# Groups of seven products: the seventh product's weight split issued behind the third product's

## The chip, the cores and the metric

The kernel runs on one core of one Trainium2 chip. The metric is device time in microseconds (us) of one execution; lower is better. A profiled execution of the kernel before is shown below, and times are compared as medians.

## The reference

One layer of a hybrid encoder, 256 rows by 2048 columns, all float32: a half-weight SwiGLU block, a mixing block (a diagonal state-space head group and a stick-breaking attention head group side by side), a second half-weight SwiGLU block, and a gated per-layer embedding.

```python
x = x + 0.5 * swiglu(rms_norm(x, ffn1_norm), w_gate, w_up, w_down)      # d_ff = 5632
h = rms_norm(x, mix_norm);  u, q, k, v = split(h @ w_in)
x = x + concat(rms_norm(s5(u)), rms_norm(attention(q, k, v))) @ w_out
x = x + 0.5 * swiglu(rms_norm(x, ffn2_norm), ...)
x = x + rms_norm((p @ w_ple_proj) * sigmoid(rms_norm(x, ple_norm) @ w_ple_gate))

def swiglu(h, w_gate, w_up, w_down):
    return (silu(h @ w_gate) * (h @ w_up)) @ w_down
```

The change touches only the two SwiGLU blocks.

## The kernel before

**Matrix products in two halves.** Each float32 weight tile is split into a high part (a cast on ScalarE, line 181) and a low part (source minus high part, on VectorE, line 184). A product is then three runs of matmuls on TensorE: high activations with high weights, low with high (lines 494 and 495 for a product of a group), and high with low (line 497). Each weight tile of a split is 128 partitions by 1024 elements and serves six matmuls of 128x512 in a group's product: four that need the high part, then two that need the low part. In the ordinary blocks (`gemm_half`, lines 322, 323 and 327) one split serves twelve.

**Groups of seven products.** For most of the two SwiGLU blocks, `Seven.chunk` computes a 2 by 2 block product (two halves of the contraction by two column blocks) with seven products instead of eight. It loads two raw weight tiles, `raw` (line 511), whose halves are b11, b21 (first tile) and b12, b22 (second tile). VectorE forms three sums (line 501): t1 = b11 + b12, t2 = t1 + b22, t4 = t2 + b21. A transfer issued by GpSimd (line 525) adds b22 onto b12 in place, in on-chip memory; it may start only after t1 has read b12. The products are then traced in this order: 1 (weights b11), 5 (t1), 6 (t2), 4 (t4), 2 (b21), 3 (b22), 7 (b12 after the transfer). So the seventh product's split waits for the transfer, and the fourth product's split waits for the last sum. The kernel has 40 such groups; the text numbers them 1 to 40 by the transfers of line 525 in order of time. "P4" is the product numbered 4 of a group, and so on.

**What sets the order.** The code traces instructions; a scheduler then puts each engine's instructions into one fixed order, and each engine works that list strictly in order, waiting at the head of it. Weight parts go through small rings of buffers: four pairs `whi`/`wlo`, and in these phases three pairs `shi`/`slo`, used in turn (`weight_pair`, line 284). Between groups, `column` computes ordinary quarter products (its matmuls are those of lines 322, 323 and 327), and `step()` lets side work go on (line 592: a copy from an accumulator; lines 593, 594, 598, 601, 627 and 629: the combination of the seven accumulators and the gate; line 216: a transposition).

## Time and profile before

| | before |
|---|---|
| median of 3 runs | 1828.03 us (1827.74 to 1829.2) |
| the profiled execution's own time | 1829.07 us |
| its span, first to last instruction | 1827.3 us |
| TensorE matmuls busy | 1817.7 us (99%) |
| VectorE busy | 1518.4 us (83%) |
| ScalarE busy | 1048.0 us (57%) |
| mean granted TensorE clock | 0.998 |

Busy time of matmuls includes overlap: one 128x512 matmul is shown as lasting 0.39 us, while the next one starts 0.23 us after it. A gap of TensorE is therefore read from the starts of its rows, not from its busy share. A row of the timeline gives the start, the duration, engine, line, operation, output <- input, shape and count, and in brackets the idle time before it and what ended that.

### The profile page before, as it was taken

How to read it: one execution, taken by the hardware profiler on the slowest of the kernel's cores; microseconds unless marked ns; L12 is line 12 of the kernel's file. 1: busy time of each engine (PE TensorE's matmuls, PEld its weight loads, DVE VectorE, ACT ScalarE, POOL GpSimd, SP SyncE). 2: the span in 40 equal slices, each digit the busy share in tenths (PEclk: the TensorE clock that was granted, in tenths of full speed). 3: DMA queues.
4: the chain of work that ended last, by engine and by line, in shares of the span. 5: the costliest groups of instructions: out<-in, count | busy, mean ns of one | idle time of the engine just before them, and what ended most of it. 6: DMA issues, size and time to landing. Idle time of an engine off the chain costs nothing.

```text
span 1827.3 us, 24177 instructions
## 1 busy us (share of the span) xinstructions
PE 1817.7 (99%) x8954; PEld 1504.9 (82%) x8954; DVE 1518.4 (83%) x1773; ACT 1048.0 (57%) x1220; POOL 101.0 (6%) x156
## 2 busy tenths in 40 slices
PE   9999999999999999999999999999999999999998
PEld 7888888888888888888898888888878888888887
DVE  8966759999898885697567899999989999888565
ACT  7444445655565665456695566555555556556554
POOL 0010000000000001010021000000000010000000
PEclk9999999999999999999999999999999999999999
DMA  9899877787777677674646788887777787667563
GB/s 328 282 286 281 247 226 231 235 246 220 254 246 238 189 250 229 186 252 156 220 149 213 241 280 234 265 258 222 241 220 236 237 274 241 226 202 250 172 217 127
DMA packets 234407, 425.27 MB, mean 233 GB/s; under 512 B 24272, under 2 KB 48240, under 8 KB 234128
## 3 DMA queue, kind: packets, MB, share of 16 engines
q1 hardware_dynamic: 223872, 390.06, 64.9%
q0 software_dynamic: 9696, 32.25, 8.1%
q8 instruction: 70, 1.15, 0.3%
q10 hardware_dynamic: 720, 1.41, 0.2%
q14 instruction: 49, 0.40, 0.1%
HBM read 372.41 MB, written 10.88 MB: 210 GB/s over the span
## 4 chain that ended last, share of the span: by engine, by line
PE 98%; DMA 1%; DVE 0%; ACT 0%; issue 0%; SPq 0%; ACTq 0%; DVEq 0%
PE acc L322 18%; PE acc L323 18%; PE acc L327 18%; PE aux L323 7%; PE aux L327 7%; PE aux L322 7%; PE acc L497 4%; PE acc L495 4%; PE acc L494 4%; PE aux L497 3%; PE aux L495 3%; PE aux L494 3%; DMA raw<-raw 1%; PE aux L1142 0%; PE acc L1398 0%; PE acc L1393 0%
## 5 line engine op out<-in xcount | busy, mean ns | idle before, releaser
L184 DVE TENSOR_TENSOR wlo<-raw,whi 128x1024 fp32r<-128x1024 f32 x486 | 589.0, 1224 | 179.3 <-ACT whi L181 177.9
L181 ACT CAST whi<-raw 128x1024 fp32r<-128x1024 f32 x486 | 505.3, 1050 | 352.5 <-PE acc L323 234.7
L322 PE MATMUL acc<-whi,nhi 128*128 128x512 f32 x1052 | 412.4, 392 | 0.9 <-ACT whi L181 0.4
L323 PE MATMUL acc<-whi,nlo 128*128 128x512 f32 x1052 | 409.6, 389 | 0.0
L327 PE MATMUL acc<-wlo,nhi 128*128 128x512 f32 x1052 | 288.8, 389 | 0.0
L184 DVE TENSOR_TENSOR slo<-raw,shi 128x1024 fp32r<-128x1024 f32 x180 | 219.2, 1218 | 32.7 <-ACT shi L181 31.3
L322 PEld LDWEIGHTS acc<-whi,nhi 128*128 128x128 f32 x1052 | 197.6, 188 | 43.9 <-ACT whi L273 1.4
L181 ACT CAST shi<-raw 128x1024 fp32r<-128x1024 f32 x180 | 188.7, 1050 | 76.1 <-DMA raw<-in_ffn_w_down 22.8
L327 PEld LDWEIGHTS acc<-wlo,nhi 128*128 128x128 f32 x1052 | 197.5, 188 | 41.1
L323 PEld LDWEIGHTS acc<-whi,nlo 128*128 128x128 f32 x1052 | 197.6, 188 | 40.1
L181 ACT CAST whi<-sum 128x1024 fp32r<-128x1024 f32 x68 | 71.6, 1053 | 136.5 <-DVE sum L501 129.9
L181 ACT CAST shi<-sum 128x1024 fp32r<-128x1024 f32 x52 | 54.8, 1053 | 85.4 <-DVE sum L501 83.0
L501 DVE TENSOR_TENSOR sum<-sum,raw 128x1024 f32<-128x1024 f32 x80 | 97.6, 1220 | 0.7
L525 POOL DMA_DIRECT2D raw<-raw x40 | 34.7, 868 | 955.3 <-DVE sum L501 657.6
L184 DVE TENSOR_TENSOR wlo<-sum,whi 128x1024 fp32r<-128x1024 f32 x68 | 83.1, 1221 | 2.4 <-ACT whi L181 1.6
L184 DVE TENSOR_TENSOR slo<-sum,shi 128x1024 fp32r<-128x1024 f32 x52 | 63.5, 1221 | 2.4 <-ACT shi L181 1.9
L322 PE MATMUL aux<-whi,hhi 128*128 128x512 f32 x168 | 65.4, 389 | 0.0
L323 PE MATMUL aux<-whi,hlo 128*128 128x512 f32 x168 | 65.4, 389 | 0.0
L323 PE MATMUL acc<-whi,hlo 128*128 128x512 f32 x160 | 62.3, 390 | 0.0
L322 PE MATMUL acc<-whi,hhi 128*128 128x512 f32 x160 | 62.2, 389 | 0.0
L322 PE MATMUL aux<-whi,nhi 128*128 128x512 f32 x156 | 60.7, 389 | 0.0
L323 PE MATMUL aux<-whi,nlo 128*128 128x512 f32 x156 | 60.7, 389 | 0.0
(375 smaller groups left out, 3200.2 us busy)
## 6 DMA issues: line engine op xcount, KB each, us to landing
raw<-in_ffn_w_up SPq DMA_DIRECT2D x88, 1024.0 KB, 6.1
raw<-in_ffn_w_down SPq DMA_DIRECT2D x88, 1024.0 KB, 5.3
raw<-in_ffn_w_gate SPq DMA_DIRECT2D x86, 1024.0 KB, 8.0
raw<-in_w_in SPq DMA_DIRECT2D x32, 1024.0 KB, 5.8
raw<-raw POOLq DMA_DIRECT2D x40, 512.0 KB, 5.9
raw<-in_w_out SPq DMA_DIRECT2D x16, 1024.0 KB, 5.2
raw<-in_w_ple_gate SPq DMA_DIRECT2D x16, 1024.0 KB, 5.3
hT<-mid SPq DMA_DIRECT2D x160, 64.0 KB, 4.3
```

Source lines behind the costliest of these rows:

```text
L181: copy = nc.scalar.copy(hi, src)
L184: nc.vector.tensor_tensor(out=lo, in0=src, in1=hi.bitcast(F32), op=ALU.subtract)
L322: nc.tensor.matmul(ps[t], lhsT=lh, rhs=hi[:, j, cols], start=start and j == 0, stop=False)
L323: nc.tensor.matmul(ps[t], lhsT=ll, rhs=hi[:, j, cols], start=False, stop=False)
L327: nc.tensor.matmul(ps[t], lhsT=lh, rhs=lo[:, j, cols], start=False, stop=stop and j == 1)
L494: nc.tensor.matmul(ps, lhsT=lh[j], rhs=hi[:, j], start=begin and j == 0, stop=False)
L495: nc.tensor.matmul(ps, lhsT=ll[j], rhs=hi[:, j], start=False, stop=False)
L497: nc.tensor.matmul(ps, lhsT=lh[j], rhs=lo[:, j], start=False, stop=z in final and j == 1)
L501: nc.vector.tensor_tensor(out=t, in0=x, in1=y, op=ALU.add)
L525: nc.gpsimd.dma_start(b12, b22, accum_op=ALU.add)
```

## The change

`split` now returns its two instructions, `product` keeps them, and `chunk` takes those of the third product and traces the seventh product inside two blocks that put the instructions of ScalarE behind the third product's cast and those of VectorE behind the third product's subtraction. Nothing is computed differently; the number of instructions on each engine is the same.

```diff
     def split(hi, lo, src, scale=None, pinned=False):
         if scale is None:
             copy = nc.scalar.copy(hi, src)
...
-            nc.vector.tensor_tensor(out=lo, in0=src, in1=hi.bitcast(F32), op=ALU.subtract)
+            rest = nc.vector.tensor_tensor(out=lo, in0=src, in1=hi.bitcast(F32), op=ALU.subtract)
+            return copy.ins, rest.ins
...
         def product(self, z, left, src, final):
             hi, lo = weight_pair()
-            split(hi, lo, src)
+            self.last = split(hi, lo, src)
...
             self.product(2, whole(1, 0), b21, final)
             self.product(3, summed(3), b22, final)
+            copied, rest = self.last
             step()
-            self.product(7, summed(2), b12, final)
+            with tc.issue_after(copied), tc.issue_after(rest):
+                self.product(7, summed(2), b12, final)
```

In 35 of the 40 groups ScalarE cast the seventh product's weights behind the third's already. The final order differs in few places: ScalarE's in groups 1, 15, 24, 28 and 29 and (one cast and one copy exchanged) behind group 31, VectorE's around groups 1, 24, 28 and 29, TensorE's in groups 24 and 28. GpSimd's and SyncE's orders are the same throughout.

Group 29, ScalarE, before. Here `raw_11502` in `shi_11571<-raw_11502` is b12 (P7), `sum_11539` is t4 (P4), and `whi_11561<-raw_11502` reads b22 (P3); `shi_11551` is P2 and `sum_11527` is t2 (P6).

```order
L181 CAST shi_11551<-raw_11500 128x1024
L181 CAST whi_11529<-sum_11527 128x1024
L181 CAST shi_11571<-raw_11502 128x1024
L181 CAST whi_11541<-sum_11539 128x1024
L181 CAST whi_11561<-raw_11502 128x1024
L181 CAST whi_11583<-raw_11581 128x1024
```

The same place now:

```order
L181 CAST shi_11551<-raw_11500 128x1024
L181 CAST whi_11529<-sum_11527 128x1024
L181 CAST whi_11541<-sum_11539 128x1024
L181 CAST whi_11561<-raw_11502 128x1024
L181 CAST shi_11571<-raw_11502 128x1024
L181 CAST whi_11583<-raw_11581 128x1024
```

P7's cast moved from ahead of P4's and P3's to behind both. VectorE's subtractions `slo_11572`, `wlo_11542` and `wlo_11562` moved in the same way.

Group 1, ScalarE, before: `whi_2687` is P2, `whi_2708` is P7, `whi_2720` belongs to the ordinary product that follows, `shi_2677` is P4 and `shi_2697` is P3.

```order
L181 CAST whi_2664<-sum_2662 128x1024
L181 CAST whi_2687<-raw_2633 128x1024
L181 CAST whi_2708<-raw_2635 128x1024
L181 CAST whi_2720<-raw_2718 128x1024
L181 CAST shi_2677<-sum_2675 128x1024
L181 CAST shi_2697<-raw_2635 128x1024
```

The same place now:

```order
L181 CAST whi_2664<-sum_2662 128x1024
L181 CAST whi_2687<-raw_2633 128x1024
L181 CAST shi_2677<-sum_2675 128x1024
L181 CAST shi_2697<-raw_2635 128x1024
L181 CAST whi_2708<-raw_2635 128x1024
L181 CAST whi_2720<-raw_2718 128x1024
```

P4's and P3's casts moved ahead of P7's and of the following product's. On VectorE, P7's subtraction moved behind those of P4 and P3.

Group 24, VectorE, before: `wlo_10742` is P2, `slo_10731` is P4, `slo_10753` is P3; the two rows of `h_10349` combine the column block before.

```order
L501 TENSOR_TENSOR sum_10728<-sum_10715,raw_10686 128x1024
L627 TENSOR_TENSOR h_10349<-aux_10420,h_10349 128x1024
L184 TENSOR_TENSOR wlo_10742<-raw_10686,whi_10741 128x1024
L629 SCALAR_TENSOR_TENSOR h_10349<-h_10349,sm_9066,sg_10348 128x512 x2
L184 TENSOR_TENSOR slo_10731<-sum_10728,shi_10730 128x1024
L184 TENSOR_TENSOR slo_10753<-raw_10688,shi_10752 128x1024
```

The same place now (three lines further on in the file after the edited ones):

```order
L502 TENSOR_TENSOR sum_10728<-sum_10715,raw_10686 128x1024
L630 TENSOR_TENSOR h_10349<-aux_10420,h_10349 128x1024
L184 TENSOR_TENSOR slo_10731<-sum_10728,shi_10730 128x1024
L632 SCALAR_TENSOR_TENSOR h_10349<-h_10349,sm_9066,sg_10348 128x512 x2
L184 TENSOR_TENSOR wlo_10742<-raw_10686,whi_10741 128x1024
L184 TENSOR_TENSOR slo_10753<-raw_10688,shi_10752 128x1024
```

P4's and P2's subtractions have changed places. Group 28 reads the same with other numbers, and in both groups TensorE's two matmuls on P4's low part, which stood behind the first matmul of P2, now stand ahead of it.

## The prediction

> **What bounds the kernel now.** I read the page first, parts 1 and 4.

> ```profile
> PE 1817.7 (99%) x8954; PEld 1504.9 (82%) x8954; DVE 1518.4 (83%) x1773; ACT 1048.0 (57%) x1220; POOL 101.0 (6%) x156
> ...
> PE 98%; DMA 1%; DVE 0%; ACT 0%; issue 0%; SPq 0%; ACTq 0%; DVEq 0%
> ```

> The chain that ended last is TensorE's own work for 98% of the span. No matmul is added or removed, so the change can give back only time in which TensorE stood still or ran slowly, and can cost only by making it stand still somewhere. Second view: who TensorE waited for.

> ```profile
> PE acc L494 <- ACT whi L181: 1.9, 1, 1.9
> ...
> PE aux L497 <- DVE wlo L184: 0.4, 1, 0.4
> ```

> The longest wait of the execution is a single one, 1.9 us for a cast on ScalarE. Third view: TensorE's timeline, searched for starts that lie further apart than usual. Around that wait (group 29) it reads:

> ```profile
> 1339.58 0.39 PE L494 MATMUL acc<-whi,hhi 128*128 128x512 f32 x1
> ...
> 1343.21 0.61 PE L497 MATMUL aux<-wlo,nhi 128*128 128x512 f32 x2
> 1345.70 0.50 PE L494 MATMUL acc<-whi,hhi 128*128 128x512 f32 x1 [1.87 <-ACT whi L181]
> ...
> 1347.14 1.22 PE L497 MATMUL acc<-wlo,hhi 128*128 128x512 f32 x2 [0.25 <-DVE wlo L184]
> ...
> 1350.65 0.39 PE L494 MATMUL aux<-whi,nhi 128*128 128x512 f32 x1
> ...
> 1353.40 0.39 PE L322 MATMUL aux<-whi,nhi 128*128 128x512 f32 x1
> ```

> From 1339.58 to 1343.21 sixteen matmuls start, so the undisturbed distance is 3.63/16 = 0.227 us. From 1343.21 to 1353.40 there are 26 starts (two of P6, six each of P4, P2, P3, P7), which should take 26 x 0.2267 = 5.89 us and took 10.19. Group 29 therefore loses **4.30 us**, far more than the 1.9 us in the table of waits: 2.57 us up to 1347.14 (3.93 us for six starts worth 1.36), and 1.73 us after it. The second piece is the clock. Busy time by stretch, with the granted clock in the column behind the count:

> ```profile
> 1343.40:1347.10 3.70, 1.63 (x6) 1.00 0.44 161
> 1347.10:1350.50 3.40, 3.35 (x8) 0.50 0.27 42
> ```

> Right behind the stall TensorE is granted half its clock for 3.4 us, and gets eight matmuls done where fifteen would fit.

> Why the cast was late is on ScalarE's and VectorE's timelines:

> ```profile
> 1335.62 1.06 ACT L181 CAST whi<-sum 128x1024 fp32r<-128x1024 f32 x1 [0.19 <-DVE sum L501]
> 1343.65 1.04 ACT L181 CAST shi<-raw 128x1024 fp32r<-128x1024 f32 x1 [6.97 <-DMA raw<-raw]
> 1344.60 1.04 ACT L181 CAST whi<-sum 128x1024 fp32r<-128x1024 f32 x1
> 1345.55 1.99 ACT L181 CAST whi<-raw 128x1024 fp32r<-128x1024 f32 x2
> ```

> ```profile
> 1338.92 1.22 DVE L501 TENSOR_TENSOR sum<-sum,raw 128x1024 f32<-128x1024 f32 x1
> 1344.73 1.23 DVE L184 TENSOR_TENSOR slo<-raw,shi 128x1024 fp32r<-128x1024 f32 x1 [4.59 <-ACT shi L181]
> 1345.87 1.22 DVE L184 TENSOR_TENSOR wlo<-sum,whi 128x1024 fp32r<-128x1024 f32 x1
> 1347.01 2.36 DVE L184 TENSOR_TENSOR wlo<-raw,whi 128x1024 fp32r<-128x1024 f32 x2
> ```

> ScalarE stood 6.97 us at the head of its list, before P7's cast, until the adding transfer had landed. P4's cast, the next in the list, had its source (t4) at 1338.92 + 1.22 = 1340.14, but ran at 1344.60. VectorE stood 4.59 us for the same reason.

> **Group 29, the first term.** ScalarE's list now has P4, P3, P7. P4's cast can start at about 1340.2 and end at 1341.2; TensorE wants it at 1343.21 + 2 x 0.2267 = 1343.66. VectorE's subtraction then ends at about 1342.5; its first matmul is due four starts later, at 1344.57. P3's cast ends at about 1342.2 and is due at 1346.38. So P4 has a cover of 2.4 and 2.1 us, and the 4.30 us go. What is late next is P7 itself: its cast still waits for the transfer until 1343.65 and ends at 1344.69, its subtraction ends at 1344.73 + 1.23 = 1345.96; due at 1347.74 and 1348.65, so 3.05 and 2.69 us are left. Behind the waiting cast stand the next ordinary product's casts. They used to start behind three casts from 1343.65, and now start behind one, 1.9 us earlier. If the transfer lands over 2.7 us later than here, TensorE waits for the excess.

> Is the landing an accident of this execution? Part 6 of the page, and the adding transfer of the stretch 1333 to 1345 alone:

> ```profile
> raw<-raw POOLq DMA_DIRECT2D x40, 512.0 KB, 5.9
> ```

> ```profile
> DMA to landing us min/median/max: 9.5/9.5/9.5
> ```

> 9.5 us against a median of 5.9: the transfer was slow here. Weight loads go out ahead of it from SyncE's fixed list, so I expect much the same in every execution. But a landing about 2 us earlier would leave little of the stall, and that is a rival below.

> [...]

> **Group 1, the second term.** The same fault, milder:

> ```profile
> 292.87 0.61 PE L497 MATMUL aux<-wlo,hhi 128*128 128x512 f32 x2
> 293.44 0.50 PE L494 MATMUL acc<-shi,nhi 128*128 128x512 f32 x1
> ...
> 294.71 0.74 PE L497 MATMUL acc<-slo,nhi 128*128 128x512 f32 x2
> ...
> 296.65 0.39 PE L494 MATMUL aux<-shi,hhi 128*128 128x512 f32 x1
> ```

> ```profile
> 290.44 2.00 ACT L181 CAST whi<-raw 128x1024 fp32r<-128x1024 f32 x2 [1.31 <-PE acc L495]
> 292.35 1.04 ACT L181 CAST shi<-sum 128x1024 fp32r<-128x1024 f32 x1
> ```

> ```profile
> 289.35 1.22 DVE L501 TENSOR_TENSOR sum<-sum,raw 128x1024 f32<-128x1024 f32 x1
> ```

> 292.87 to 296.65 is 3.78 us for 14 starts worth 3.17: **0.61 us** lost. P4's cast (292.35) ended at 293.39, just before its matmul. Two casts stood ahead of it that now stand behind; t4 is ready at 290.57, so the cast can end at about 291.65, the subtraction at 292.9, against dues of 293.33 and 294.23. Covers of 1.7 and 1.3 us: all 0.61 us go. P7's cast moves from 290.44 to about 292.6, and is used from about 297.4 on.

> **The other moved places, at nothing.** In group 15 P7's cast, which waited for a buffer, goes behind P4's and P3's; in group 31 one cast passes the copy of line 592.

> ```profile
> 1043.30 1.05 ACT L181 CAST whi<-raw 128x1024 fp32r<-128x1024 f32 x1 [1.49 <-PE aux L327]
> ```

> ```profile
> 1048.40 1.22 DVE L184 TENSOR_TENSOR wlo<-raw,whi 128x1024 fp32r<-128x1024 f32 x1
> ...
> 1394.40 0.69 DVE L593 TENSOR_TENSOR h<-aux,sg 128x512 f32<-128x512 f32 x1 [2.12 <-PE aux L497]
> ```

> P7's cast in group 15 can be later by two casts (1.9 us) and still end at about 1046.3, ahead of its subtraction at 1048.40. The copy's reader in group 31 (line 593) waits 2.12 us for TensorE anyway, which covers the one cast. Should either cover be gone, the lateness beyond it is TensorE's. Group 24 (28 is its twin) moves P2's subtraction back:

> ```profile
> 1240.02 1.41 DVE L629 SCALAR_TENSOR_TENSOR h<-h,sm,sg 128x512 f32<-128x512 f32 x2
> 1241.35 1.22 DVE L184 TENSOR_TENSOR slo<-sum,shi 128x1024 fp32r<-128x1024 f32 x1
> ```

> ```profile
> 1243.92 0.61 PE L497 MATMUL acc<-wlo,hhi 128*128 128x512 f32 x2
> ```

> P2's low part now takes the slot at 1241.35 and ends at 1242.57; its matmuls are at 1243.92. Cover 1.35 us; without it every late microsecond is one of TensorE's. P4's low part takes P2's earlier slot. Its cast no longer stands behind P7's, so nothing is lost there.

> **What is given back.** TensorE moves ahead by 4.30 us in group 29; VectorE doesn't. From 1345.96 on VectorE works without a break, and only the two subtractions now done ahead of P7's (2 x 1.14 = 2.27 us) are saved, and a short gap in group 30 (its P7 subtraction is the row at 1370.44, its first matmul the one at 1373.35):

> ```profile
> 1363.15 1.22 DVE L184 TENSOR_TENSOR slo<-raw,shi 128x1024 fp32r<-128x1024 f32 x1
> 1364.48 1.22 DVE L627 TENSOR_TENSOR h<-aux,h 128x1024 f32<-128x1024 f32 x1
> ...
> 1370.44 1.18 DVE L184 TENSOR_TENSOR wlo<-raw,whi 128x1024 fp32r<-128x1024 f32 x1
> ```

> ```profile
> 1373.35 0.62 PE L497 MATMUL aux<-wlo,nhi 128*128 128x512 f32 x2
> ```

> Line 627 starts 1.33 us after the row ahead, against 1.14 without a gap: 0.19 us of waiting for TensorE, which falls away. VectorE is thus 2.46 us earlier at 1370.44, TensorE 4.30 at 1373.35. The margin between them was 1373.35 - 1371.62 = 1.73 us and becomes 1.73 - (4.30 - 2.46) = -0.11: P7 of group 30 waits a little. With some 0.14 us for the restart I take **0.25 us**. Its bounds: 0, if VectorE is 0.11 us earlier than I count (no gain is possible, since TensorE doesn't wait there now); and, if VectorE were not earlier at all, 4.30 - 1.73 = 2.57 us of stall, 0.14 for the restart and 1.73 for the clock, 4.4 in all. I stay near the lower end, since the two subtractions stand ahead in VectorE's list.

> **The sum.** 4.30 + 0.61 - 0.25 = 4.66 us. The profiled execution would go from 1829.07 to 1824.4 us (span 1827.3 to 1822.6). It ran 1.04 us above the median of the timed runs; against that median, 1828.03 - 4.66 gives **1823.4 us**. I take the median, since it is what will be compared, and treat the 1.04 us as uncertainty on how much of the stall a timed run has.

> **Rivals.**

> (a) *The slow clock is not the wait's.* If the 3.4 us of half clock come for another reason, they stay: 4.66 - 1.73 = 2.93 us gain, 1825.1 us. Against: it follows directly on the only long stall. [...] 5%.

> (b) *The timed runs stall less.* With the transfer landing at its median, group 29 loses little, and the gain is 0.61 us and a rest of up to 2.6: 1825.4 to 1827.4 us. For: the profiled execution is 1.04 us above the median. Against: 1829.07 lies within the range of the timed runs, and the loads ahead of the transfer are the same each time. 12%.

> (c) *VectorE becomes the bound in group 30.* If it is later than I count by 1 to 2 us, TensorE stalls there instead, perhaps with the clock: 1 to 3.6 us given back, so 1824.4 to 1827.0 us. For: VectorE has no break from 1344.73 on. 12%.

> (d) *Slower: P2's low part is late in groups 24 and 28.* It now stands behind two combinations (line 629) that wait for TensorE through line 627. If it comes over 1.35 us later, TensorE stalls in both groups. With 3.4 us of stall and the clock's 1.73 in each, 2 x 5.13 = 10.3 us are lost against 4.9 us gained: 1833.4 us. It outweighs the gain from some 2 us beyond the cover. Against: the rows ahead of it keep their order. 6%.

> That the order isn't changed where it matters is excluded by the lists: P4's cast does stand ahead of P7's in groups 1 and 29.

> **How the numbers follow.** The forecast has 65%. A measurement of this kernel can tell about 0.2% (3.7 us) from no change. The forecast lies beyond that, at 0.25%; (a), (b) and (c) lie within it; (d) beyond it on the other side. So faster 0.65, same 0.29, slower 0.06. The range goes from 1822.5 (nothing given back, and the stall as large in the timed runs as in the profile, with the runs' own spread of 0.3 us below) to 1826.2, which takes in (a), most of (c) and a part of (b).

> **What would show it.** Right: TensorE's starts in group 29 run on at 0.227 us from P6 to P7, no stretch at half clock there, ScalarE casting `whi<-sum` at once after the sum with a short wait on the transfer behind it; no wide starts around 293; a new small wait for a subtraction in P7 of group 30. Wrong: a wait of a microsecond or more at a low part in groups 24, 28 or 30; a stretch at half clock that remains; the first long idle time of ScalarE still ahead of a cast from `sum`.

## The result, and the profile after

The changed kernel takes 1824.1 us (median, 1823.26 to 1825.79), the kernel before, run beside it, 1827.56 us (1825.54 to 1829.2). The ratio is 0.9981, with a 95% interval of 0.9973 to 0.9988: faster by 3.5 us, 0.19%. The profiled execution went from 1829.07 to 1823.56 us, its span from 1827.3 to 1821.8 us, which is 5.5 us and thus more than the medians differ.

The first part of the changed kernel's page, and below it the two rows of its table of waits for TensorE (total, count, longest, in us) that stand in place of those shown before:

```profile
span 1821.8 us, 24180 instructions
...
PE 1814.3 (100%) x8954; PEld 1504.3 (83%) x8954; DVE 1518.4 (83%) x1773; ACT 1048.4 (58%) x1220; POOL 100.7 (6%) x156
```

```profile
PE acc L323 <- ACT whi L181: 0.4, 1, 0.4
PE aux L498 <- DVE wlo L184: 0.4, 1, 0.4
```

The work is the same; the single wait of 1.9 us for a cast is gone, and nothing of its size has come in its place. Group 29 on TensorE's timeline, from P6's low part to the first matmul of line 323 behind P7 (lines 495, 498 and 323 were 494, 497 and 322):

```profile
1342.59 0.62 PE L498 MATMUL aux<-wlo,nhi 128*128 128x512 f32 x2
1343.04 0.39 PE L495 MATMUL acc<-whi,hhi 128*128 128x512 f32 x1
...
1347.12 0.39 PE L495 MATMUL aux<-shi,nhi 128*128 128x512 f32 x1
...
1348.48 0.39 PE L323 MATMUL aux<-whi,nhi 128*128 128x512 f32 x1
```

The 26 starts now take 1348.48 - 1342.59 = 5.89 us, exactly the undisturbed time, where they took 10.19. The stretches of that time, TensorE's busy time and count, then the granted clock:

```profile
1343.00:1347.00 4.00, 4.00 (x19) 1.00 0.61 176
1347.10:1350.50 3.40, 3.40 (x16) 1.00 1.05 401
```

The half clock is gone with the stall. ScalarE's timeline and VectorE's, in that order, show why:

```profile
1339.56 1.05 ACT L181 CAST whi<-sum 128x1024 fp32r<-128x1024 f32 x1 [3.49 <-DVE sum L502]
1340.51 1.05 ACT L181 CAST whi<-raw 128x1024 fp32r<-128x1024 f32 x1
1342.06 1.06 ACT L181 CAST shi<-raw 128x1024 fp32r<-128x1024 f32 x1 [0.50 <-DMA raw<-raw]
```

```profile
1338.30 1.22 DVE L502 TENSOR_TENSOR sum<-sum,raw 128x1024 f32<-128x1024 f32 x1
1340.65 1.22 DVE L184 TENSOR_TENSOR wlo<-sum,whi 128x1024 fp32r<-128x1024 f32 x1 [1.12 <-ACT whi L181]
...
1343.15 1.23 DVE L184 TENSOR_TENSOR slo<-raw,shi 128x1024 fp32r<-128x1024 f32 x1
```

The sum t4 ends at 1339.52, P4's cast starts 0.04 us later, P3's follows, and only P7's waits for the adding transfer: 0.50 us of idle time where it had been 6.97. Group 1, TensorE and ScalarE:

```profile
292.97 0.62 PE L498 MATMUL aux<-wlo,hhi 128*128 128x512 f32 x2
...
296.15 0.39 PE L495 MATMUL aux<-shi,hhi 128*128 128x512 f32 x1
```

```profile
290.71 1.05 ACT L181 CAST shi<-sum 128x1024 fp32r<-128x1024 f32 x1 [1.47 <-DVE sum L502]
```

P4's cast starts at 290.71 instead of 292.35, and the 14 starts take 3.18 us instead of 3.78: nothing is lost there any more.

### The profile page after: what moved, and what is told of

Read it like the earlier page. It is cut to its first block, busy times and chain, and to the rows that moved or that the text cites. A ratio compares the mean times of both kernels' runs of the same rounds, so it can differ in the third digit from the quotient of the medians.

```text
span 1821.8 us, 24180 instructions
## 1 busy us (share of the span) xinstructions
PE 1814.3 (100%) x8954; PEld 1504.3 (83%) x8954; DVE 1518.4 (83%) x1773; ACT 1048.4 (58%) x1220; POOL 100.7 (6%) x156
## 3 DMA queue, kind: packets, MB, share of 16 engines
q10 hardware_dynamic: 720, 1.41, 0.2%
## 4 chain that ended last, share of the span: by engine, by line
PE 99%; DMA 0%; ACT 0%; DVE 0%; SPq 0%; issue 0%; DVEq 0%
PE acc L323 18%; PE acc L324 18%; PE acc L328 18%; PE aux L324 7%; PE aux L328 7%; PE aux L323 7%; PE acc L498 4%; PE acc L496 4%; PE acc L495 4%; PE aux L498 3%; PE aux L496 3%; PE aux L495 3%; PE aux L1145 0%; PE acc L1401 0%; PE acc L1396 0%; PE acc L1392 0%
## 5 line engine op out<-in xcount | busy, mean ns | idle before, releaser
L184 DVE TENSOR_TENSOR wlo<-raw,whi 128x1024 fp32r<-128x1024 f32 x486 | 588.9, 1223 | 182.8 <-ACT whi L181 181.2
L181 ACT CAST whi<-raw 128x1024 fp32r<-128x1024 f32 x486 | 505.3, 1050 | 349.9 <-PE acc L324 236.5
L184 DVE TENSOR_TENSOR slo<-raw,shi 128x1024 fp32r<-128x1024 f32 x180 | 219.1, 1217 | 26.7 <-ACT shi L181 26.4
L181 ACT CAST shi<-raw 128x1024 fp32r<-128x1024 f32 x180 | 188.9, 1050 | 69.2 <-DMA raw<-in_ffn_w_down 20.8
L181 ACT CAST whi<-sum 128x1024 fp32r<-128x1024 f32 x68 | 71.6, 1054 | 140.4 <-DVE sum L502 129.9
L181 ACT CAST shi<-sum 128x1024 fp32r<-128x1024 f32 x52 | 54.8, 1054 | 90.3 <-DVE sum L502 85.5
L184 DVE TENSOR_TENSOR wlo<-sum,whi 128x1024 fp32r<-128x1024 f32 x68 | 83.0, 1221 | 3.8 <-ACT whi L181 3.1
L184 DVE TENSOR_TENSOR slo<-sum,shi 128x1024 fp32r<-128x1024 f32 x52 | 63.5, 1221 | 1.0 <-ACT shi L181 0.5
## 6 DMA issues: line engine op xcount, KB each, us to landing
raw<-raw POOLq DMA_DIRECT2D x40, 512.0 KB, 5.8
```

What stands on the lines that cost most here:

```text
L181: copy = nc.scalar.copy(hi, src)
L184: rest = nc.vector.tensor_tensor(out=lo, in0=src, in1=hi.bitcast(F32), op=ALU.subtract)
```

## The experiments

The theory: the gain is the two stalls at the head of ScalarE's list, in groups 29 and 1. The rivals: the half clock has another reason, the stall depends on when the transfer lands, or the gain is spread over the other moved places. One number is read in the same way from every profile below, TensorE's time beyond 0.2267 us per start, by place (us):

| kernel | span | group 1 | group 16 | group 24 | group 29 | group 30 | 1660 to 1800 us |
|---|---|---|---|---|---|---|---|
| before | 1827.3 | 0.61 | 0.74 | 0 | 4.29, half clock | 0 | 0.60 |
| before_a (before, again) | 1828.2 | 1.06 | 0.87 | 0.88 | 2.65 | 0 | 1.27 |
| before_b (before, again) | 1825.3 | 0.55 | 0.80 | 0 | 2.32 | 0 | 0.66 |
| before_late | 1825.2 | 0.55 | 0.84 | 0 | 1.85 | 0 | 0.64 |
| not29 | 1824.3 | 0 | 0.77 | 0 | 2.48 | 0 | 0.18 |
| only29 | 1822.3 | 0.57 | 0.91 | 0 | 0 | 0 | 0 |
| only29_a (again) | 1823.7 | 0.85 | 0.84 | 0 | 0 | 0 | 0.38 |
| only29_b (again) | 1822.9 | 0.60 | 0.87 | 0.25 | 0 | 0 | 0 |
| after | 1821.8 | 0 | 0.74 | 0 | 0 | 0 | 0 |
| after_late | 1822.2 | 0 | 0.49 | 0 | 0 | 0 | 0 |
| turn_one | 1823.6 | 0 | 0.54 | 0 | 0 | 0.31 | 0.77 |
| after_later | 1825.2 | 0 | 0.78 | 0 | 0 | 2.57 | 0.32 |

Besides, every profile loses 1.9 to 2.7 us in its first 13 us, where the kernels don't differ, and turn_one another 1.0 us at 1406 to 1410.

**One part alone, and all but that part.** The change in group 29 only (only29), and everywhere but there (not29, with `!= 29`):

```diff
+            groups[0] += 1
-            with tc.issue_after(copied), tc.issue_after(rest):
+            with ExitStack() as behind:
+                if groups[0] == 29:
+                    behind.enter_context(tc.issue_after(copied))
+                    behind.enter_context(tc.issue_after(rest))
                 self.product(7, summed(2), b12, final)
```

> The change in group 29 alone (35 groups keep their order anyway; groups 1, 15, 24 and 28 go back to the order before). If the gain is ScalarE standing before the seventh product's cast in group 29, this kernel has nearly all of it: 2.6 to 3.2 us below before, about 0.6 us above the changed kernel, with TensorE's starts wide only around 293 us (0.61 us). If the gain is spread over the other moved places, it is less than 1.5 us below before.

> The change everywhere but in group 29. By the theory of group 29 it gains the 0.61 us of group 1 and no more, 0.3 to 0.9 us below before, and its trace still shows ScalarE idle for some 6 to 7 us before P7's cast in group 29, TensorE waiting 1 to 2 us for P4's cast and perhaps a stretch at half clock. By the rival (gain spread over the places) it is over 1.5 us below before.

only29 took 1826.1 us (1824.12 to 1827.23) and not29 1826.09 us (1824.51 to 1827.81), beside 1827.57 us of the kernel before: both ratios are 0.9992, with an interval of 0.9983 to 1.0. The profiles split as the theory says: only29 loses nothing in group 29 and 0.57 us in group 1, not29 nothing in group 1 and 2.48 us in group 29. TensorE in group 29 of not29 (lines 497 and 500 are the high and low part of a product here):

```profile
1342.48 0.61 PE L500 MATMUL aux<-wlo,nhi 128*128 128x512 f32 x2
1344.71 0.50 PE L497 MATMUL acc<-whi,hhi 128*128 128x512 f32 x1 [1.61 <-ACT whi L181]
```

The same wait as before the change, but this time without half clock behind it. The timed runs don't tell the two parts apart: each brings 1.5 us by its median, where the profiles say 2.5 and 0.6, and the intervals (0 to 3.1 us) hold both. Both forecasts of the time were missed (2.6 to 3.2 us for only29, 0.3 to 0.9 for not29), and by the medians alone the gain looks spread: only29's 1.47 us lies under 1.5, as that rival had it, and not29's 1.48 us just misses being over 1.5, as that rival had it there. That the larger part of the time comes from group 29 is therefore shown by the profiles alone.

**The kernel before and only29 again**, without an edit, to see how much of group 29's stall belongs to one execution:

> The kernel before once more, for another profiled execution. If what differs between executions is group 29, its loss varies: 1 to 4.3 us, with the landing of the adding transfer (7.6 to 9.2 us after its issue so far) and with or without a stretch at half clock, and the execution's time follows it one for one; group 1 loses 0.5 to 0.7 us each time, since what ScalarE waits for there is TensorE. If the executions differ elsewhere, group 29 stays within 0.5 us while the time moves by over 1 us.

> As the other repeat of the kernel before: group 29 loses 1 to 4.3 us, group 1 0.5 to 0.7 us, and the time of the execution follows group 29.

> The change in group 29 alone, for another profiled execution. The timed executions had a median of 1826.1 us where the profiled one had 1824.1. If group 1 is worth more than the 0.6 us of its profile, its loss here is 1 to 2.5 us in one of the repeats, with a stretch at half clock. If not, it is 0.5 to 0.7 us and the difference lies at the start, at the end or nowhere in particular.

> As the other repeat of the change in group 29 alone: 0.5 to 0.7 us lost in group 1 if that place is the same each time, 1 to 2.5 us if it is what varies.

They took 1829.97, 1827.12, 1825.43 and 1824.71 us. The stall comes back in each execution with the old order (2.65 and 2.32 us) and in none with the new one. But the time of an execution does not follow group 29, though that had been expected: before_a and before_b differ by 2.85 us in all, but by only 0.33 us in that group. Group 1 varies more than expected as well (1.06 us in before_a, 0.85 in only29_a).

One of these executions shows a place that the theory had left out. In group 24, too, P4's cast stood behind P7's in the old order. In before_a the adding transfer of that group took 6.5 us to land (4.5 in the first profile). ScalarE, then TensorE:

```profile
1241.18 1.06 ACT L181 CAST whi<-raw 128x1024 fp32r<-128x1024 f32 x1 [3.95 <-DMA raw<-raw]
1242.14 1.03 ACT L181 CAST shi<-sum 128x1024 fp32r<-128x1024 f32 x1
```

```profile
1243.23 0.50 PE L494 MATMUL acc<-shi,hhi 128*128 128x512 f32 x1 [0.46 <-ACT shi L181]
```

TensorE loses 0.88 us there. In only29_b, which keeps the old order in group 24, a transfer of 5.9 us goes with a loss of 0.25 us; the other five profiles with that order have transfers of 4.5 to 5.4 us and lose nothing. With the new order none of five profiles loses anything there, though the transfer takes 6.1 us in after_later. So the change seems to remove a third stall too, one that comes only when that transfer lands late; no run tests this place alone.

The half clock does not come back: of the five profiles with group 29's old order only the first has it there. In that one it lasts 3.413 us, and in the three profiles read for it the changes of granted clock lie whole multiples of that length apart. In the first profile the end of the half clock, at 1350.54, and the next change, at 1825.0, are 139 of them apart (474.45 us); in before_a the first record of full clock begins at 4.86 us and the change at the end comes at 1827.58, 534 of them later; in the changed kernel's profile the two changes, at 6.14 and 1818.61 us, are 531 of them apart. In stretches of that length counted from these changes, TensorE's busy time, count and clock in the kernel before, first profile, and in before_a:

```profile
1343.72:1347.13 3.41, 1.31 (x5) 1.00 0.37 138
1347.13:1350.54 3.41, 3.40 (x8) 0.50 0.27 44
```

```profile
1342.88:1346.29 3.41, 2.81 (x13) 1.00 0.94 294
1346.30:1349.71 3.41, 1.96 (x7) 1.00 0.07 26
1349.71:1353.12 3.41, 3.41 (x16) 1.00 0.56 166
```

A window with 1.31 us of busy time was followed by one at half clock, a window with 1.96 us was not. The stalls are alike (2.57 and 2.65 us). In the first profile nearly all of it fell into one window; in before_a, before_b and not29 it was cut in two, and before_late's, which lies mostly in one, was shorter (1.85 us). The least busy windows of these four have 1.96 to 2.27 us, and the clock stays. At the end of the executions, behind other matmuls, windows with as much as 1.61 us were followed by half clock (before_b):

```profile
1818.75:1822.16 3.41, 1.61 (x5) 1.00 0.48 176
1822.17:1825.30 3.13, 0.00 (x0) 0.50 0.42 145
```

That the busy share of the window decides is read from these rows and not tested by a run. By this reading the 1.73 us are the stall's, but only in an execution whose windows happen to lie so.

**The transfer issued later, in the old order.** GpSimd gets a copy and three fills ahead of group 29's adding transfer:

```diff
             t1 = self.add(b11, b12)
-            nc.gpsimd.dma_start(b12, b22, accum_op=ALU.add)
+            late[0] += 1
+            if late[0] == 29:
+                slack = com("sq")
+                slow = pin(nc.gpsimd.tensor_copy(slack, t1[:, 0, :]))
+                for _ in range(3):
+                    slow = pin(nc.gpsimd.memset(slack, 0.0))
+            pin(nc.gpsimd.dma_start(b12, b22, accum_op=ALU.add))
```

> Before, with one copy and three fills of 128x512 put on GpSimd ahead of group 29's adding transfer, so that it starts 2 to 4 us later; all other lists are those of before. If TensorE's stall there is the landing of the transfer through ScalarE's list, each microsecond of delay is one of TensorE: 2 to 4 us slower than before, and the stall of 2 us grows to 4 to 6 us, with half clock behind it. If the stall is P4's sum or VectorE being busy, the time stays within 0.7 us of before.

It took 1826.37 us (1825.62 to 1827.41), ratio 0.9992 (0.9983 to 1.0001), so not slower. GpSimd's issue, in the kernel before and in before_late, then the transfer's way to landing and P7's cast in before_late:

```profile
1333.96 0.88 POOL L525 DMA_DIRECT2D raw<-raw  x1 [17.97 <-DVE sum L501]
```

```profile
1337.22 0.88 POOL L533 DMA_DIRECT2D raw<-raw  x1 [0.25 <-issue]
```

```profile
raw<-raw POOLq DMA_DIRECT2D x1, 512.0 KB, 5.7
```

```profile
1343.06 1.05 ACT L181 CAST shi<-raw 128x1024 fp32r<-128x1024 f32 x1 [5.68 <-DMA raw<-raw]
```

The transfer went out 3.26 us later and took 5.7 us instead of 9.5: it landed 0.6 us earlier, and group 29 lost 1.85 us. The expectation missed because the landing it was about did not come later, so this run does not decide between its two theories. While the transfer was held back, other transfers kept the DMA engines busy (0.95 of the time from 1335 to 1337); that the landing follows from those more than from the issue fits the pair, but no run tests it.

**The same delay in the changed kernel.**

```diff
+            if late[0] == 29:
+                slack = com("sq")
+                slow = pin(nc.gpsimd.tensor_copy(slack, t1[:, 0, :]))
+                for _ in range(3):
+                    slow = pin(nc.gpsimd.memset(slack, 0.0))
```

> The changed kernel with the same late transfer in group 29. By the theory P7's cast has some 3 us of cover, so a delay of 2 to 3 us costs 0 to 0.5 us against the changed kernel and the kernel stays 3 to 3.5 us below before; beyond 3 us of delay TensorE waits for the excess, now at P7. If VectorE were the bound in group 30, the late subtraction of P7 would move the whole of its list and cost 1.5 us or more, with waits for low parts in group 30.

It took 1824.0 us (1823.72 to 1825.33), ratio 0.9983 (0.9974 to 0.9992). Since the delay did not move the landing to a later time, this only repeats the changed kernel's result; the cover of P7 was not put to the test. A longer delay did that, with eight fills:

```diff
-                for _ in range(3):
+                for _ in range(8):
```

> The changed kernel with one copy and eight fills ahead of group 29's adding transfer, so that it is issued about 6 us late, at 1339 us, when the weight loads ahead of it are done. It should then land 4.5 to 5.5 us later, at 1343.7 to 1344.7 us, 2 to 3 us after that of the changed kernel. By the theory P7's cover of about 3 us takes it: group 29 loses 0 to 0.5 us at P7, none at P4, and the kernel stays 3 us or more below before. If VectorE were the bound behind it, group 30 would lose 1 us or more at its low parts.

It took 1826.83 us (1826.46 to 1827.56), ratio 0.9997 (0.9987 to 1.0006): the gain is gone. The issue and the way to landing, then VectorE, then TensorE in after_later (line 500 is a product's low part):

```profile
1339.35 0.87 POOL L534 DMA_DIRECT2D raw<-raw  x1 [0.25 <-issue]
```

```profile
raw<-raw POOLq DMA_DIRECT2D x1, 512.0 KB, 5.9
```

```profile
1346.47 1.23 DVE L184 TENSOR_TENSOR slo<-raw,shi 128x1024 fp32r<-128x1024 f32 x1 [2.96 <-ACT shi L181]
...
1364.91 1.21 DVE L184 TENSOR_TENSOR wlo<-sum,whi 128x1024 fp32r<-128x1024 f32 x1
```

```profile
1364.22 0.39 PE L498 MATMUL acc<-whi,hlo 128*128 128x512 f32 x1
1366.18 0.74 PE L500 MATMUL acc<-wlo,hhi 128*128 128x512 f32 x2 [1.57 <-DVE wlo L184]
...
1370.96 0.73 PE L500 MATMUL aux<-wlo,nhi 128*128 128x512 f32 x2 [0.37 <-DVE wlo L184]
```

P7's subtraction starts 3.32 us later than in the changed kernel and still meets its matmuls. Behind it VectorE works without a break for 18 us, so the lateness arrives whole in group 30: P4's subtraction (the row at 1364.91, from a sum) starts 3.31 us later than in the changed kernel and ends at 1366.12, its matmul waits, and with P7's of group 30 that makes 2.57 us. The first of the two theories was right that group 29 itself loses nothing, but its forecast of the time fell; the second held.

**The loss in group 16.** One wait for a low part remains in the changed kernel:

```profile
1082.69 0.73 PE L498 MATMUL aux<-wlo,nhi 128*128 128x512 f32 x2 [0.37 <-DVE wlo L184]
```

There VectorE does transpositions (line 217) ahead of P7's subtraction. The experiment puts the subtraction ahead of one pair:

```diff
-                put_off(2, turned, hp, f, hh)
+                put_off(2 if f else 3, turned, hp, f, hh)
```

> The changed kernel with one more exchange: in group 16 VectorE's subtraction for P7 goes ahead of the two transpositions of line 217 that stood before it (1.2 us); all other lists stay. In the profile of the changed kernel TensorE loses 0.6 to 0.7 us there, the last wait for a split in the groups. If VectorE's list alone holds P7 there, this loss goes to 0 and the time is 0.6 to 0.7 us below the changed kernel (about 4 us below before). If VectorE's lag only moves on, it comes back at the next low parts and the time stays.

It took 1823.65 us (1823.18 to 1825.39), ratio 0.9982 (0.9973 to 0.9991), not to be told from the change alone. TensorE at the same place in turn_one:

```profile
1081.99 0.62 PE L498 MATMUL aux<-wlo,nhi 128*128 128x512 f32 x2
...
1083.70 0.73 PE L328 MATMUL acc<-slo,nhi 128*128 128x512 f32 x2 [0.20 <-DVE slo L184]
```

P7's low part is on time, and the next low part is late in its place. The loss is 0.54 us against 0.74, but after_late, without this exchange, has 0.49, so no part of the difference can be put down to it. This fits VectorE being behind there as a whole: the exchange changed which matmul waits.

## Why the prediction was right, and where its size was off

**The mechanism held, step by step.** P4's cast starts as soon as its source is there, and all of group 29's loss and all of group 1's go. only29 and not29 take the two losses away one at a time in their profiles. One sign of being wrong was worded too loosely: ScalarE still stands idle ahead of a cast from `sum`, for 3.49 us before P4's cast of group 29, but that time ends with the sum itself (the cast starts 0.04 us behind it), and not with the transfer.

**The failed term is group 29's, 4.30 us.** It was read from one execution, and that execution had the half clock. Without it the stall of the old order is 1.85 to 2.65 us in four profiles. Of the 33 timed runs of the kernel before beside only29, at least 17 had no such stretch: their mean granted clock rounds to 1.000, and by an estimate from the first profile one such stretch alone, 3.41 us at half clock in 1827, would leave 0.9991. With the middle values of the table, 2.5 us in group 29 and 0.6 in group 1, 3.1 us are explained of the 3.5 measured. The rest may be group 24 in some executions, the last column (0.18 to 1.27 us with group 29's old order, 0 to 0.77 with the new one, by a cause that was not found), or nothing, since the gain itself is known only to within 2.2 to 4.9 us. The forecast of 4.66 us was thus 1.2 us too large, mostly because the row of the half clock was counted as certain. That the time came out closer, 1824.1 for 1823.4 us, is luck in part: the median of before was 1827.56 us beside the changed kernel, 0.47 us below the one that the forecast started from.

**Rival (a), the slow clock is not the wait's,** was right in that the 1.73 us are not to be counted in every run, wrong in its reason: in the one profile with half clock there, it comes behind the stall, in the window after the one that the stall had filled.

**Rival (b), the timed runs stall less,** comes near in size: 0.61 and up to 2.6 us, where 3.5 were measured. The transfer's landing in group 29 is not what makes the difference, as that rival had it; it takes 9.2 to 9.6 us there in before_a, before_b, not29 and turn_one too.

**What is given back: 0 instead of 0.25 us.** The transfer landed after 8.6 us in the changed kernel's profile, not 9.5. Group 30's P7 there, VectorE and TensorE:

```profile
1366.41 1.18 DVE L184 TENSOR_TENSOR wlo<-raw,whi 128x1024 fp32r<-128x1024 f32 x1
```

```profile
1368.42 0.62 PE L498 MATMUL aux<-wlo,nhi 128*128 128x512 f32 x2
```

The margin is 1368.42 - 1367.59 = 0.83 us instead of -0.11. The difference is the transfer: in the stretch's own time, counted from P6's low part (1343.21 before, 1342.59 after), P7's cast is 0.97 us earlier than in the old order. In turn_one, where the transfer took 9.6 us, group 30 does lose 0.31 us at this place. The term's working holds for the landing it assumed. Its 0.14 us for the restart are what the profile before shows in group 16, behind TensorE's wait of 0.40 us there: the five starts from 1083.26 to 1084.53 us took 1.27 us and were worth 1.13.

**Rival (c), VectorE becomes the bound in group 30,** did not come about, but after_later shows its mechanism and price: a landing some 3 us later gives back 2.57 us. Its place is right as well, except that P4's low part is late ahead of P7's. In group 29 itself P7 was still on time, so that the cover to watch is VectorE's unbroken list and not P7's own.

**Rival (d), P2's low part late in groups 24 and 28,** did not happen. Group 24, VectorE and TensorE:

```profile
1240.76 1.22 DVE L184 TENSOR_TENSOR wlo<-raw,whi 128x1024 fp32r<-128x1024 f32 x1
```

```profile
1243.31 0.62 PE L498 MATMUL acc<-wlo,hhi 128*128 128x512 f32 x2
```

The subtraction ends at 1241.98, which leaves 1.33 us; 1.35 had been worked out. What the prediction missed in group 24 is on the other side: it saw that P4's cast no longer stands behind P7's, but put the gain at nothing, where before_a's late transfer costs the old order 0.88 us.

## What to carry to other kernels

Look for an instruction that waits for a transfer at the head of an engine's list with ready ones behind it. Here the profile shows that as 6.97 us of ScalarE's idle time ahead of one cast, while the next one, whose source was there at 1340.14, ran at 1344.60; the loss stands at TensorE, which waited 1.87 us for that next cast. Read such a loss from the distance of starts, and from several executions of the old kernel before counting what looks like its consequence: here a clock drop worth 1.73 us came in one of five, and a loss in group 24 in two of seven. When the stall goes, look for the next list without a gap that the same late transfer feeds: here 3.32 us of lateness were still 3.31 us some 18 us later.
